# Key norms along turned rows, layer 1 turned by transposes, two bank halves in the scan, another order at its seam

## The chip, the cores and the metric

The kernel runs on one core of a Trainium2 chip. The metric is the device time of one execution in microseconds, as a median of several runs. The engines are TensorE (PE; its weight loads are PEld), VectorE (DVE), ScalarE (ACT), GpSimd (POOL) and SyncE (SP), which issues most of the DMAs.

## The reference

One pass through two layers, on 512 latent tokens and 256 context tokens, D = 1024, all in fp32.

```python
# both layers: scale, shift and gate come from the conditioning vectors by ada_w
u = rms_norm(h, norm_g[i]) * (1.0 + scale) + shift
h = h + gate * mixer(u)

# layer 0, gated DeltaNet in both directions; q, k, v = silu(conv(u @ w_in)), z = the gate path
q = l2_norm(q); k = l2_norm(k)     # x * rsqrt(sum(x * x) + 1e-6) over the 128 of a head
# per chunk of 64 tokens: T = inverse of (I + A), QK = decayed q k^T, and a state S for each head
v_new = T @ (v - k S); o = q S + QK @ v_new; S = S * g + k^T v_new
y = (rms_norm(o) * silu(z)) @ w_out

# layer 1, attention of 8 query heads on 2 key/value heads, with rotary rows; only the latents go on
y_lat = (softmax(q k^T) v * silu(z)) @ w_out
return rms_norm(h_lat, final_norm_g)
```

Layer 0 has 8 key heads and 8 query heads of 128, and 16 value heads of 128.

## The kernel before, in words

Large products run as three passes in a reduced fp32 format: each operand is split into a high part and the rest, and high by high, high by rest and rest by high are summed in PSUM. Times below are us from the start of the profiled span.

**The front (0 to 145)** makes the layer norms, the conditioning and the 8 key heads. For a key head, PE makes the projection in two pieces, of 512 and 256 tokens (`k_products`, L491), with channels on the partitions; ACT and DVE make the convolution and the silu (`sil_k`, 128 channels x 768 tokens). The norm of each token is a sum over partitions. So ACT squares all of it (`k_squared`, L532), PE sums the squares with twelve products by a column of ones, each an fp32 matmul of two instructions (`k_summed`, L540), DVE adds epsilon while it copies the sums out (`k_sums`, L545), and once for two heads DVE takes 1/sqrt (`k_roots`, a chain of small operations, L178 to L183). PE turns the head to tokens on partitions by six transposes (`k_turned`, L461), ACT scales each 128x128 of it by its tokens' roots while it copies it out of PSUM (`k_scaled`, L558, six instructions), the result is stored, and PE turns it back for the second form of the keys (`k_back`, L567; copied by ACT in `k_kept`).

**The heads of q, v and z (145 to 549)** are products of the same kind (`gemm_part`, L929), among them the decay matrices and the inverses T of every chunk (L713 to L892). The last of these are `pn` and `pw` (L846, L864). In both stretches the order of the work on each engine is not written out: each step is a `K(engine, cost, due, function, after=..., takes=..., holds=...)`, and `written_out` (L1113) places them one by one: by the earliest start that the engine, its operands and the free buffers in `pool_of` (L1053) allow, then by due time. `T0` (L1134) and `STEP` set the due times of the key heads, `SLOT` those of the others. Costs only set the order: on the chip every engine takes its own queue in this order and waits on semaphores.

**The scan (549 to 725)** has 48 steps x, four for each chunk, with four heads of both directions each. `products(x)` (L1546 on) makes `ks` on PE (k S and q S), `r` on DVE (L1567, four pieces) and `o` on ACT (L1570, four pieces). `solve(x)` makes `pr` = T r on PE (L1590), and ACT copies it out as `vn` (L1592). `update(x)` makes `pq` = QK vn (L1616), which DVE adds to the output `O` (L1630), and the state's change `su` (L1624), which DVE adds to `S`. `pr` and `pq` have one PSUM buffer of two banks each, of which half is used. A step x of the loop runs `products(x)`, `solve(x - 1)`, `update(x - 2)`. From x = 43 the steps of layer 0's output norm are put between them; `chain` holds the small operations of its roots, and `out_gated`, `out_cast` and `out_rest` (L1703 to L1723) turn the first unit of the output projection into its high part and rest.

**The output projection of layer 0 (725 to 874)** has 32 units n (L1744 three passes each). From n = 24 on, one k at a time, the context tokens are made ready for layer 1: `u_block` is `u_turn` (L1882), then `u_split` (L1887 to L1889). `u_turn` norms and turns in one: a product of `h` with a diagonal matrix `diag1` of the tokens' roots, an fp32 matmul of two instructions for each 128x128. `u_split` applies scale and shift in PSUM on DVE, ACT casts the high part out, and DVE subtracts it. `norm1_diag` makes the diagonal matrices.

**Layer 1 (874 to the end)** begins with `kv`, the keys and values (L2036): six blocks k of the context, then `u_block` for k = 0 and 1 of the latents, then two context blocks, then for each k `u_block(k + 2)` and the latents' `kv_block(k)`. Attention, its gates and the last projection follow. From the scan on the order on PE, DVE and ACT is the order of the code.

Of the kernel before, what the change touches and what calls it, by code (L numbers as in the profile page):

```python
# [8 lines left out]
F32 = mybir.dt.float32  # L9
# [8 lines left out]
P = 128  # L18
# [68 lines left out]
def backbone(tc, a, out):  # L87
# [380 lines left out]
    kw, khl, kbank, kacc, ksil, ksq, kps, kroot, ktr, ktok, kpb = ({} for _ in range(11))  # L468
# [33 lines left out]
    def k_centre(h, i):  # L502
        c0, n = SPAN[i]
        if i == 0:
            open_late()
            kacc[h] = room["late"].tile([P, NTOK], F32, tag="acc", name=f"acc_k{h}", bufs=2)
        S.activation(kacc[h][:, c0:c0 + n], kbank[h, i][:, :n], AF.Copy, scale=cwv[:, 2, 8 + h:9 + h])
# [22 lines left out]
    def k_squared(h):  # L530
        ksq[h] = room["late"].tile([P, NTOK], F32, tag="sq", name=f"sq_k{h}", bufs=2)
        S.activation(ksq[h], ksil[h], AF.Square)  # L532

    def k_summed(h):
        ps = kps[h] = pa.tile([P, 512], F32, tag="gq", name=f"ss_k{h}")
        sq = ksq.pop(h)
        for t in range(NT):
            for hf in range(2):
                c0 = t * P + hf * 64
                T.matmul(ps[hf * 64:hf * 64 + 64, t:t + 1], sq[:, c0:c0 + 64], ones, start=True, stop=True)  # L540

    def k_sums(h):
        if h % 2 == 0:
            kroot[h // 2] = ap_.tile([P, 2 * NT], F32, tag="kss", name=f"kss{h}")
        V.tensor_scalar(kroot[h // 2][:, h % 2 * NT:(h % 2 + 1) * NT], kps.pop(h)[:, 0:NT], EPS, None, ALU.add)  # L545

    def k_roots(h):
        rsqrt(kroot[h // 2], add=False)

# [3 lines left out]
    def k_scaled(h):  # L553
        kt = ktok[h] = room["late"].tile([P, NT, P], F32, tag="tok", name=f"kt{h}", bufs=2)
        pt, r = ktr.pop(h), kroot[h // 2]
        for i, t0, n in halves():
            for t in range(t0, t0 + n):
                S.activation(kt[:, t], pt[i][:, t - t0], AF.Copy, scale=r[:, h % 2 * NT + t:h % 2 * NT + t + 1])  # L558
# [481 lines left out]
    class Piece:  # L1040
        def __init__(self, engine, cost, due, fn, *args, after=(), takes=(), holds=(), lands=0.0, since=0.0, slack=None, behind=(), port=0, sent=0.0, far=0.0):
# [5 lines left out]
            for x, owner in holds:  # L1047
# [8 lines left out]
                                          ("lacc", 2), ("lsil", 4), ("lsq", 2), ("lkb", 2), ("ltok", 2))}  # L1056
# [77 lines left out]
    T0 = 140  # L1134
# [94 lines left out]
    def k_finish(h, e, t0, sown, r_, kown):  # L1229
# [11 lines left out]
    for h in range(QH):  # L1241
# [28 lines left out]
        if h % 2 == 0:  # L1270
            kown, first_of, left_ = ks_, (h, e, t0, sq_[0]), []
            continue
# [1287 lines left out]
```

## Time and profile before

| | |
|---|---|
| median of 3 runs | 1163.69 us (1161.95, 1163.69, 1169.8) |
| the profiled execution, its span | 1162.45 us, 1160.7 us |
| busy share: PE, DVE, ACT, POOL | 97%, 69%, 63%, 51% |
| mean granted TensorE clock | 0.994 |
| PE idle in 0-145, 145-549, 549-725 us | 14.5, 4.7, 4.3 us |
| PE idle in 725-874, 874-917, 917-1127 us, and after | 0.1, 1.7, 3.0, 10.3 us |

The page of the profile gives busy time of each engine and, in 40 slices, the busy share in tenths. A group row reads: line, engine, operation, out<-in, shape, count | busy us, mean ns of one | idle time just before, and what ended it. A timeline row is start, duration, engine, line, operation, out<-in, count; an fp32 matmul or transpose of one call may stand in it as two instructions. Matmuls overlap: the pitch between starts, not the duration, is what each costs PE. The list of waits gives the engine's idle time by what it waited for. A row of windows gives for a stretch its length and then the busy time of PE, PEld, DVE, ACT and POOL, each with its instructions, then the granted TensorE clock, the DMA share and GB/s.

### The profile page before, as it was taken

The numbers are of one execution on the slowest core, as the hardware profiler recorded it, in microseconds if no ns is written. First come the engines' busy times: TensorE is split into PE (matmuls) and PEld (weight loads), VectorE is DVE, ScalarE is ACT, GpSimd is POOL, SyncE is SP. The second block draws the span as 40 slices with busy tenths as digits, with TensorE's granted clock in tenths as the row PEclk, the third lists the DMA queues.
The fourth block names the chain that finished last, engine by engine and source line by source line (L and its number), as shares of the span: only waits on it lengthen the run. The fifth ranks groups of instructions, "written<-read, shape, count | busy, mean of one in ns | idle before, by whom it ended". The sixth has DMA issues, their size and how long they took to land. (4 is left out here: it accounts for less than half of the span.)

```text
span 1160.7 us, 27663 instructions
## 1 busy us (share of the span) xinstructions
PE 1122.1 (97%) x10751; PEld 917.8 (79%) x10751; DVE 796.3 (69%) x1651; ACT 735.2 (63%) x1918; POOL 589.1 (51%) x509
## 2 busy tenths in 40 slices
PE   5999999999999999999999999999999999999996
PEld 2777788888888888887666666788887889999885
DVE  4786465688897888873787888455657467666646
ACT  4545544576876888855789888875753246666731
POOL 0554000149999989930585597556635143130810
PEclk9999999999999999999999999999999999999998
DMA  9577854757647867566988983686844112101323
GB/s 368 200 270 267 302 150 133 220 154 210 180 139 231 265 212 227 171 223 210 268 242 242 285 257 99 205 221 189 250 114 139 34 55 73 37 19 56 109 73 91
DMA packets 117141, 208.73 MB, mean 180 GB/s; under 512 B 12145, under 2 KB 76818, under 8 KB 111762
## 3 DMA queue, kind: packets, MB, share of 16 engines
q1 hardware_dynamic: 97074, 195.32, 54.4%
q10 hardware_dynamic: 19936, 11.64, 3.4%
q8 instruction: 85, 1.39, 0.5%
q14 instruction: 46, 0.38, 0.1%
HBM read 166.16 MB, written 40.67 MB: 178 GB/s over the span
## 5 line engine op out<-in xcount | busy, mean ns | idle before, releaser
L1744 PE MATMUL po<-woh,y 128*128 128x512 f32 x384 | 129.7, 401 | 0.1
L1573 POOL TENSOR_TENSOR S<-S,glb 128x512 f32<-128x512 f32 x80 | 81.8, 1043 | 89.1 <-PE ks L1564 88.8
L1682 POOL TENSOR_TENSOR wol<-wo,woh 128x1024 fp32r<-128x1024 f32 x32 | 77.2, 2412 | 56.0 <-ACT woh L1675 52.7
L813 POOL TENSOR_TENSOR X<-X,tmp 128x62 f32<-128x62 f32 (+15 forms) x93 | 98.1, 1054 | 7.3
L812 POOL TENSOR_TENSOR tmp<-L,X 128x62 f32<-128x62 f32 (+15 forms) x93 | 95.3, 1024 | 6.7
L929 PE MATMUL g_z<-uh,wh_z 128*128 128x512 f32 (+1 forms) x256 | 89.2, 348 | 2.0 <-DVE sil_v L963 1.9
L944 DVE SCALAR_TENSOR_TENSOR acc_v<-g_v,cwv,acc_v 128x510 f32<-128x510 f32 (+3 forms) x128 | 78.0, 614 | 16.4 <-ACT acc_v L936 12.9
L929 PE MATMUL g_v<-uh,wh_v 128*128 128x512 f32 (+1 forms) x256 | 88.0, 344 | 0.0
L929 PE MATMUL g_v<-uh,wl_v 128*128 128x512 f32 (+1 forms) x256 | 86.2, 337 | 1.3 <-issue 1.3
L929 PE MATMUL g_z<-uh,wl_z 128*128 128x512 f32 (+1 forms) x256 | 86.8, 339 | 0.0
L929 PE MATMUL g_z<-ul,wh_z 128*128 128x512 f32 (+1 forms) x256 | 86.7, 339 | 0.0
L929 PE MATMUL g_v<-ul,wh_v 128*128 128x512 f32 (+1 forms) x256 | 86.1, 336 | 0.0
L1744 PEld LDWEIGHTS po<-woh,y 128*128 128x128 f32 x384 | 72.3, 188 | 15.7 <-ACT y L1717 0.3
L1744 PE MATMUL po<-wol,y 128*128 128x512 f32 x192 | 75.4, 393 | 0.0
L1710 DVE SCALAR_TENSOR_TENSOR pt<-pt,og,z 128x128 f32<-128x128 f32 x96 | 34.4, 358 | 33.6 <-PE pt L1701 31.3
L918 POOL TENSOR_TENSOR wl_z<-w_z,wh_z 128x1024 fp32r<-128x1024 f32 x3 | 8.0, 2677 | 96.1 <-ACT wh_z L915 96.1
L1638 DVE TENSOR_TENSOR S<-su,S 128x512 f32<-128x512 f32 x80 | 51.5, 686 | 6.7 <-PE su L1624 4.5
L929 PEld LDWEIGHTS g_z<-uh,wh_z 128*128 128x128 f32 x256 | 48.9, 191 | 8.0 <-DVE sil_v L963 2.2
L1564 PE MATMUL ks<-S,ck 128*64 128x256 f32 x352 | 55.2, 392 | 0.0
L929 PEld LDWEIGHTS g_v<-uh,wl_v 128*128 128x128 f32 x256 | 48.5, 189 | 6.7 <-issue 1.5
L1567 DVE SCALAR_TENSOR_TENSOR r<-ks,negV,cv 128x128 f32<-128x128 f32 x176 | 52.4, 345 | 1.1
L929 PEld LDWEIGHTS g_z<-uh,wl_z 128*128 128x128 f32 x256 | 48.8, 191 | 5.4
(452 smaller groups left out, 3345.0 us busy)
## 6 DMA issues: line engine op xcount, KB each, us to landing
aw<-in_ada_late SPq DMA_DIRECT2D x16, 1024.0 KB, 8.2
wo<-in_dn_w_out SPq DMA_DIRECT2D x32, 512.0 KB, 4.0
cv<-v_d SPq DMA_DIRECT2D x22, 512.0 KB, 8.1
aw<-in_ada_first SPq DMA_DIRECT2D x8, 1024.0 KB, 11.5
w_z<-in_dn_w_in SPq DMA_DIRECT2D x16, 512.0 KB, 5.3
w_v<-in_dn_w_in SPq DMA_DIRECT2D x16, 512.0 KB, 4.2
v_d<-vt ACTq DMA_DIRECT2D x16, 384.0 KB, 4.1
cT<-t_d SPq DMA_DIRECT2D x12, 512.0 KB, 7.7
```

Source lines behind the costliest of these rows:

```text
L812: G.tensor_tensor(tv, bcast(L[:, :, j + 1:, j], 3, j + 1), bcast(X[:, :, j, 0:j + 1], 2, n), ALU.mult)
L813: G.tensor_tensor(X[:, :, j + 1:, 0:j + 1], X[:, :, j + 1:, 0:j + 1], tv, ALU.subtract)
L918: E.tensor_tensor(split_w_[n][1], raw_w.pop(n), split_w_[n][0], ALU.subtract)
L929: T.matmul(ps[:, :m], w[:, k], u[:, k, c0:c0 + m], start=k == 0 and n_ == 0, stop=k == KT - 1 and n_ == 2)
L944: V.scalar_tensor_tensor(acc[:, c0 + lo:c0 + hi], ps[:, lo + j - 2:hi + j - 2], cwv[:, j, ct:ct + 1], acc[:, c0 + lo:c0 + hi], ALU.mult, A ...
L1564: T.matmul(ks[r0:r0 + 64, w], kq[w][:, hh, r0:r0 + 64], St[hh][:, d], start=True, stop=True)
L1567: V.scalar_tensor_tensor(r[:, 2 * j + i], ks[:, 0, i], negV[:, visit, t, h:h + 1], v[:, h], ALU.mult, ALU.add)
L1573: G.tensor_tensor(St[hh], St[hh], bcast(g_, 3, P), ALU.mult)
L1638: V.tensor_tensor(St[hh], sj, St[hh], ALU.add)
L1682: G.tensor_tensor(wl, raws.pop(n), halves[n][0], ALU.subtract)
L1710: V.scalar_tensor_tensor(pj, pj, og, raw(z, off, [[st_, 2], [1, 64]]), ALU.mult, ALU.mult)
L1744: T.matmul(acc[nh], y[i][:, j, :], ww[k][:, nh * 512:(nh + 1) * 512], start=h == 0 and x == 0, stop=h == VH - 1 and x == 2)
```

## The change

It has four parts.

1. **Key norms.** `k_summed` and `k_sums` go. The head is turned first, directly after its silu; ACT then squares each turned 128x128 out of PSUM with an accumulator, which gives the tokens' sums as a column (`k_squared`, six instructions), and copies the turned head out in two wide copies (`k_copied`). The roots follow for two heads at once, now with the epsilon (one DVE operation more), and POOL multiplies the copied head by its roots in place (`k_scaled`, 128x768). `k_back` and the rest stay. The tokens' buffers `tok` go from two to four, `T0` from 140 to 134. Since the list of steps is another, the whole order up to the scan is placed anew.
2. **Layer 1.** `h` is scaled by its roots on ACT ahead of the turn, in wide pieces (`h_columns`): the context in place, 128x512 (n = 22 and 23); the latents 128x128 for k = 0, 128x384 for k = 1 to 3, 128x512 for k = 4 to 7. `u_turn` is then a transpose, one instruction for each 128x128. Scale and shift go from DVE to ACT: one Identity writes the high part, a second one writes the full value in PSUM; DVE still subtracts. `gy` has eight buffers instead of six, which the scaled pieces share.
3. **Bank halves.** `pr` and `pq` are one tile each for the whole scan, and step x takes half x % 2 of it.
4. **Order at the seam.** At x = 47 the last step of the chain and `out_gated`, `out_cast` go from ahead of and within `products(47)` to behind `solve(46)`.

```diff
+    def k_turned(h):
+        ktr[h] = to_tokens(ksil.pop(h), f"k{h}")
+
     def k_squared(h):
-        ksq[h] = room["late"].tile([P, NTOK], F32, tag="sq", name=f"sq_k{h}", bufs=2)
-        S.activation(ksq[h], ksil[h], AF.Square)
-
-    def k_summed(h):
-        ps = kps[h] = pa.tile([P, 512], F32, tag="gq", name=f"ss_k{h}")
-        sq = ksq.pop(h)
-        for t in range(NT):
-            for hf in range(2):
-                c0 = t * P + hf * 64
-                T.matmul(ps[hf * 64:hf * 64 + 64, t:t + 1], sq[:, c0:c0 + 64], ones, start=True, stop=True)
-
-    def k_sums(h):
         if h % 2 == 0:
             kroot[h // 2] = ap_.tile([P, 2 * NT], F32, tag="kss", name=f"kss{h}")
-        V.tensor_scalar(kroot[h // 2][:, h % 2 * NT:(h % 2 + 1) * NT], kps.pop(h)[:, 0:NT], EPS, None, ALU.add)
-
-    def k_roots(h):
...
-    def k_turned(h):
-        ktr[h] = to_tokens(ksil.pop(h), f"k{h}")
...
-    def k_scaled(h):
-        kt = ktok[h] = room["late"].tile([P, NT, P], F32, tag="tok", name=f"kt{h}", bufs=2)
-        pt, r = ktr.pop(h), kroot[h // 2]
         for i, t0, n in halves():
             for t in range(t0, t0 + n):
-                S.activation(kt[:, t], pt[i][:, t - t0], AF.Copy, scale=r[:, h % 2 * NT + t:h % 2 * NT + t + 1])
+                c = h % 2 * NT + t
+                S.activation(ksq[t % 2], ktr[h][i][:, t - t0], AF.Square, accum_out=kroot[h // 2][:, c:c + 1])
+
+    def k_copied(h):
+        kt, pt = room["late"].tile([P, NT, P], F32, tag="tok", name=f"kt{h}", bufs=4), ktr.pop(h)
+        ktok[h] = kt
+        for i, t0, n in halves():
+            S.copy(kt[:, t0:t0 + n], pt[i][:, :n])
+
+    def k_roots(h):
+        rsqrt(kroot[h // 2])
+
+    def k_scaled(h):
+        kt, r = ktok[h], kroot[h // 2]
+        G.tensor_tensor(kt, kt, bcast(r[:, h % 2 * NT:(h % 2 + 1) * NT], 2, P), ALU.mult)
...
-    T0 = 140
+    T0 = 134
...
-        tu = K("PE", 0.65, t0 - 20, k_turned, h, after=[r_], takes=["tr", "tr"], holds=[("lsil", sown)], lands=0.1, slack=QUICK)
-        sc_ = K("ACT", 2.2, e + 8, k_scaled, h, after=[tu, r_], takes=["ltok"], holds=[("tr", tu), ("tr", tu), ("kss", kown)], lands=0.1)
...
+        sc_ = K("POOL", 1.85, e + 8, k_scaled, h, port=1, after=[r_, cp_], holds=[("ltok", cp_), ("kss", kown)], lands=0.1)
...
+        tu = K("PE", 0.65, t0 - 50, k_turned, h, after=si + backs.pop(h - 4, []), takes=["tr", "tr"], holds=[("lsil", sq_[0])], lands=0.1, slack=QUICK)
+        ks_ = K("ACT", 2.9, e + 6, k_squared, h, after=[tu], takes=["kss"] if h % 2 == 0 else (), holds=[("tr", tu), ("tr", tu)] + ([("kss", kown)] if h % 2 else []), lands=0.1)
+        cp_ = K("ACT", 1.0, e + 7, k_copied, h, after=[tu, ks_], takes=["ltok"], holds=[("tr", tu), ("tr", tu)], lands=0.1)
...
-        r_ = K("DVE", 2.1, e + 6, k_roots, h, port=9, after=[ks_, kown], holds=[("kss", kown)], lands=0.1)
...
+        r_ = K("DVE", 2.3, e + 6, k_roots, h, port=10, after=[ks_, kown], holds=[("kss", kown)], lands=0.1)
...
+        prq = [pcx.tile([P, 2, 4, P], F32, tag=tag, name=f"{tag}_all", bufs=1) for tag in ("pr", "pq")]
...
-            pr_ = pcx.tile([P, 2, 4, P], F32, tag="pr", name=f"pr{x}", bufs=1)
+            pr_ = prq[0][:, :, x % 2 * 2:x % 2 * 2 + 2]
...
             vn = ch.tile([P, 4, P], F32, tag="vn", name=f"vn{x}", bufs=2)
-            S.copy(vn.rearrange("p (j i) d -> p j i d", j=2), pr_[:, :, 0:2])
+            S.copy(vn.rearrange("p (j i) d -> p j i d", j=2), pr_)
...
-            po = pcx.tile([P, 2, 4, P], F32, tag="pq", name=f"pq{x}", bufs=1)
+            po = prq[1][:, :, x % 2 * 2:x % 2 * 2 + 2]
...
-        if x == 47:
-            out_gated(0, AB)
         if x < 48:
             products(x)
         if x == 45:
             out_scale(0, AB)
-        if x == 47:
-            out_cast(0, AB)
         if 0 <= x - 1 < 48:
             solve(x - 1)
         if x == 47:
+            some(chain, 99)
+            out_gated(0, AB)
+            out_cast(0, AB)
             out_rest(0, AB)
             out_scale(0, C)
         if 0 <= x - 2 < 48:
...
         if x in (43, 44, 45, 46):
-            some(chain, (3, 6, 6, 99)[x - 43])
+            some(chain, (3, 6, 6, len(chain) - 1)[x - 43])
...
+        gy = acc if inside else hpool.tile([P, 512], F32, tag="gy", name=f"gy{t}_{nh}", bufs=8)
...
-    def norm1_diag(tiles, r):
+    hn = {}
+
+    def h_columns(k0, k1, tiles, r):
         for t in tiles:
-            S.activation(diag1[t], ident, AF.Copy, scale=r[:, t - min(tiles):t - min(tiles) + 1])
+            h, m = h_t[t][:, k0 * P:k1 * P], (k1 - k0) * P
+            if t < 2:
+                y = h
+            elif k1 == 1:
+                if t == 2:
+                    hn["t"] = hpool.tile([P, 4, P], F32, tag="hn", name="hn")
+                y = hn["t"][:, t - 2]
+            else:
+                y = hpool.tile([P, 512], F32, tag="gy", name=f"hn{k0}_{t}", bufs=8)[:, 0:m]
+            S.activation(y, h, AF.Copy, scale=r[:, t - r0[t]:t - r0[t] + 1])
+            for k in range(k0, k1):
+                hn[k, t] = y[:, (k - k0) * P:(k - k0 + 1) * P]
...
         ps = trt(f"ht{k}_{j}")
         for q, t in enumerate(tiles):
-            T.matmul(ps[:, q, :], h_t[t][:, k * P:(k + 1) * P], diag1[t], start=True, stop=True)
+            T.transpose(ps[:, q, :], hn[k, t], ident)
         return ps.rearrange("p a b -> p (a b)")[:, 0:len(tiles) * P]
 
     def u_split(k, j, pv, dst):
 
-        V.tensor_scalar(pv, pv, au[1][:, j, 1, k:k + 1], au[1][:, j, 0, k:k + 1], ALU.mult, ALU.add)
-        S.copy(dst[0][:, k], pv)
+        s_, b_ = au[1][:, j, 1, k:k + 1], au[1][:, j, 0, k:k + 1]
+        S.activation(dst[0][:, k], pv, AF.Identity, bias=b_, scale=s_)
+        S.activation(pv, pv, AF.Identity, bias=b_, scale=s_)
         V.tensor_tensor(dst[1][:, k], pv, dst[0][:, k], ALU.subtract)
...
-        if n == 22:
-            norm1_diag((0, 1), r_c)
+        if n in (22, 23):
+            for k0 in (0, 4):
+                h_columns(k0, k0 + 4, (n - 22,), r_c)
...
-    norm1_diag((2, 3, 4, 5), r_l)
+    h_columns(0, 1, lat, r_l)
+    h_columns(1, 4, lat, r_l)
...
+            u_block(k + 2, 0, lat, uL)
+        if k < 2:
+            h_columns(4, 8, lat[2 * k:2 * k + 2], r_l)
         kv_block(k, (2, 3, 4, 5))
```

What the built programs show of it, in the order of the queues (numbers behind names tell tiles apart):

ACT in the front, key head 0. Before, from the square on (`sq_k`, then the six scaled copies `kt`):

```order
L532 ACTIVATE sq_k_1014<-sil_k_935 128x768
L558 ACTIVATE kt_1045<-tr_k_1016,kss_790 128x128 x4
L558 ACTIVATE kt_1045<-tr_k_1017,kss_790 128x128 x2
L507 ACTIVATE acc_k_1012<-g_k_999,cwv 128x256
L520 ACTIVATE g_k_904<-acc_k_1012 128x512
L485 CAST wh_k_1096<-w_k_881 128x1024
L576 COPY kb_1121<-kb_0_1101 128x512
L576 COPY kb_1121<-kb_0_1102 128x256
```

Now, from the first square on:

```order
L542 ACTIVATE sq_k_545,kss_698<-tr_k_672 128x128
L542 ACTIVATE sq_k_546,kss_698<-tr_k_672 128x128
L542 ACTIVATE sq_k_545,kss_698<-tr_k_672 128x128
L542 ACTIVATE sq_k_546,kss_698<-tr_k_672 128x128
L542 ACTIVATE sq_k_545,kss_698<-tr_k_673 128x128
L542 ACTIVATE sq_k_546,kss_698<-tr_k_673 128x128
L423 COPY rows_4_721<-pa_4_689 128x512
L548 COPY kt_731<-tr_k_672 128x512
L548 COPY kt_731<-tr_k_673 128x256
L485 CAST wh_k_749<-w_k_670 128x1024
```

The square of 128x768 and the six scaled copies have become six squares of 128x128 with an accumulator (`kss`) and two wide copies, which stand earlier, ahead of the roots.

DVE at the seam of scan and output projection, x = 47, from the chain's last step (`fo`) on. Before:

```order
L1486 SCALAR_TENSOR_TENSOR fo<-fo,rq 128x16
L1710 SCALAR_TENSOR_TENSOR pt_9898<-pt_9898,og,z_0_9246 128x128 x2
L1567 SCALAR_TENSOR_TENSOR r_9903<-ks_0_9905,negV,cv_9707 128x128 x2
L1567 SCALAR_TENSOR_TENSOR r_9903<-ks_1_9914,negV,cv_9707 128x128 x2
L1723 TENSOR_TENSOR y_0_0_9925<-pt_9898,y_0_0_9924 128x256
L1630 TENSOR_TENSOR O_7010<-pq_9940,O_7010 128x512
```

Now, from `r` of step 47 on:

```order
L1565 SCALAR_TENSOR_TENSOR r_9713<-ks_0_9715,negV,cv_9526 128x128 x2
L1565 SCALAR_TENSOR_TENSOR r_9713<-ks_1_9724,negV,cv_9526 128x128 x2
L1483 SCALAR_TENSOR_TENSOR fo<-fo,rq 128x16
L1708 SCALAR_TENSOR_TENSOR pt_9710<-pt_9710,og,z_0_9079 128x128 x2
L1721 TENSOR_TENSOR y_0_0_9748<-pt_9710,y_0_0_9747 128x256
L1628 TENSOR_TENSOR O_6912<-pq_all,O_6912 128x512 x2
```

`r` of step 47 has moved ahead of `fo` and the gating (`pt`), and the two additions to `O` (L1628; of `pq` of steps 45 and 46) stay behind `y`, the rest of the first unit. On PE, with the semaphores of each row, the change has there `pr` of step 47, `pq` of step 46 and the first products of the output projection:

```order
L1588 MATMUL pr_all_6943<-r47_9713,cT_11_9525 64x128 [waits DVE_49,Activation_49]
L1588 MATMUL pr_all_6943<-r47_9713,cT_11_9525 64x128
L1588 MATMUL pr_all_6943<-r47_9713,cT_11_9525 64x128 [waits DVE_49]
L1588 MATMUL pr_all_6943<-r47_9713,cT_11_9525 64x128 x3
L1588 MATMUL pr_all_6943<-r47_9713,cT_11_9525 64x128 [waits DVE_49]
L1588 MATMUL pr_all_6943<-r47_9713,cT_11_9525 64x128
L1614 MATMUL pq_all_6944<-vn46_9742,cQK_11_9527 64x128 [waits DVE_49]
L1614 MATMUL pq_all_6944<-vn46_9742,cQK_11_9527 64x128 x7
```

`pr` of step 47 still waits for ACT: the copy `vn46`, which reads the other half. `pq` of step 46 still waits for DVE: the addition just ahead of it, of `pq` of step 45, which reads the other half as well. So stand these waits through the whole scan.

PE in layer 1, the first two turns of the latents. Before:

```order
L1882 MATMUL ht_0_11662<-dn_10038,h_10023 128x128
L1882 MATMUL ht_0_11662<-dn_10039,h_10024 128x128
L1882 MATMUL ht_0_11662<-dn_10040,h_10025 128x128
L1882 MATMUL ht_0_11662<-dn_10041,h_10026 128x128
L1882 MATMUL ht_0_11670<-dn_10038,h_10023 128x128
L1882 MATMUL ht_0_11670<-dn_10039,h_10024 128x128
L1882 MATMUL ht_0_11670<-dn_10040,h_10025 128x128
L1882 MATMUL ht_0_11670<-dn_10041,h_10026 128x128
L2036 MATMUL kv_11589<-wkv_10030,uC_10032 128x512
```

Now:

```order
L1892 MATMUL ht_0_11475<-ident,hn 128x128 x4
L1892 MATMUL ht_0_11483<-ident,hn_2_11423 128x128
L1892 MATMUL ht_0_11483<-ident,hn_3_11425 128x128
L1892 MATMUL ht_0_11483<-ident,hn_4_11427 128x128
L1892 MATMUL ht_0_11483<-ident,hn_5_11429 128x128
L2048 MATMUL kv_11393<-wkv_9838,uC_9840 128x512
```

Half as many instructions, and the second turn (`ht_0_11483`) now reads the 128x384 pieces (`hn_2` to `hn_5`), which ACT makes after the four of 128x128 that the first turn reads. Both still stand ahead of the context's last two blocks of `kv`.

More of the change, by code (lines that the diff above doesn't have):

```diff
@@ L506, in k_centre @@
             kacc[h] = room["late"].tile([P, NTOK], F32, tag="acc", name=f"acc_k{h}", bufs=2)
+            if h == 0:
+                for j in range(2):
+                    ksq[j] = room["late"].tile([P, P], F32, tag=f"sq{j}", name=f"sq_k{j}")
         S.activation(kacc[h][:, c0:c0 + n], kbank[h, i][:, :n], AF.Copy, scale=cwv[:, 2, 8 + h:9 + h])
@@ L1861, in load_h @@
             dma(h_t[t][hf * 64:hf * 64 + 64, :], src[c * 64:c * 64 + 64, :])
-    diag1 = [hpool.tile([P, P], F32, tag=f"dn{t}", name=f"dn{t}") for t in range(NT)]
     def norm1_steps(tiles, nm):
```

39 lines of the change are left out of this document (18 added, 21 removed).

## The prediction

> **What bounds the kernel now.** I read the busy times first, then TensorE's list of waits, then windows and the timeline of the places that the change touches. The page begins:
>
> ```profile
> span 1160.7 us, 27663 instructions
> ## 1 busy us (share of the span) xinstructions
> PE 1122.1 (97%) x10751; PEld 917.8 (79%) x10751; DVE 796.3 (69%) x1651; ACT 735.2 (63%) x1918; POOL 589.1 (51%) x509
> ```
>
> PE has 38.6 us of idle time in the whole span. So an instruction taken off PE is worth its pitch wherever PE is never idle, and work moved to ACT, DVE or POOL is free until PE waits for it. The list of PE's waits (us in total, times, longest) has these that touch the change:
>
> ```profile
> PE pr L1590 <- ACT vn L1592: 3.0, 2, 1.7
> PE g_z L929 <- DVE sil_v L963: 1.9, 1, 1.9
> PE ht L1882 <- DVE uL L1889: 1.3, 2, 1.1
> PE g_v L929 <- issue: 1.3, 1, 1.3
> PE pw L864 <- issue: 1.0, 1, 1.0
> ```
>
> Two windows of the key heads show what PE and the others do there:
>
> ```profile
> 58.00:87.00 29.00, 29.00 (x232) 21.97 (x231) 25.95 (x52) 12.23 (x22) 16.58 (x18) 1.00 0.77 271
> 87.00:116.00 29.00, 29.00 (x240) 22.53 (x239) 19.94 (x50) 14.78 (x38) 14.09 (x31) 1.00 0.76 267
> ```
>
> PE is busy for all 29 us of both; ACT has half of the time free, POOL 12 to 15 us, DVE only 3 us in the first.
>
> **Key norms, PE: -7.0 us.** The eight groups of sums go; the turn of each head stays, only earlier. The group of sums over PE instructions, and one of the eight blocks in the timeline, between a product and the next other one:
>
> ```profile
> L540 PE MATMUL ss_k<-ones,sq_k 128*64 128x1 f32 x192 | 6.9, 199 | 0.0
> ```
>
> ```profile
> 72.85 0.28 PE L500 MATMUL g_k<-ul,wh_k 128*128 128x256 f32 x1
> 73.06 0.87 PE L540 MATMUL ss_k<-ones,sq_k 128*64 128x1 f32 x24
> 73.86 0.70 PE L431 MATMUL pg<-rows,sel 128*128 128x512 f32 x1
> ```
>
> The products before it go at a pitch of 0.12, so the next would have come at 72.97; it came at 73.86. A block costs between 0.80 (its own start to the next) and 0.89: 6.4 to 7.1 for eight. I take 7.0, near the group's 6.9 busy.
>
> What replaces them must stay hidden. ACT, by rows of the same forms:
>
> ```profile
> L532 ACT ACTIVATE sq_k<-sil_k 128x768 f32<-128x768 f32 x8 | 6.8, 846 | 2.2 <-DVE sil_k L528 2.2
> L558 ACT ACTIVATE kt<-tr_k,kss 128x128 f32<-128x128 f32 x48 | 13.3, 381 | 5.2 <-PE tr_k L461 5.2
> L1592 ACT COPY vn<-pr 128x512 f32<-128x512 f32 x48 | 28.2, 588 | 2.9 <-PE pr L1590 1.3 <-DVE sil_z L961 0.9 <-ACT O L1628 0.7
> ```
>
> A head has cost 0.85 + 13.3/8 = 2.5. Now it has six squares with an accumulator and copies of 512 and 256 columns. If a square takes no more than a scaled copy of its size with its read-out 0.1 longer (0.28 to 0.38), that is 1.7 to 2.3, with copies of 0.59 and about 0.4: 2.7 to 3.3, up to 0.8 a head more, some 6 us in a stage of 60 in which ACT is half idle. POOL's 128x768 product is new. The nearest row is the scan's 128x512:
>
> ```profile
> L1573 POOL TENSOR_TENSOR S<-S,glb 128x512 f32<-128x512 f32 x80 | 81.8, 1043 | 89.1 <-PE ks L1564 88.8
> ```
>
> By columns that is 1.6 a head. It is hidden by the products of about two heads, which the new order puts between a head's turn and its `kb`. DVE loses a copy for each head and gains an operation for each pair. So the stage's sum is PE's.
>
> **The order placed anew: 0, from -3.6 to +4.** All of the stage up to 549 is placed anew, and its waits with it; those in the list that are likely to go or come are the 1.9, 1.3 and 1.0. The 1.9 has a tail. The timeline at it, and windows behind it (granted clock third from the end):
>
> ```profile
> 341.38 0.82 PE L461 MATMUL tr_v<-ident,sil_v 128*128 128x128 f32 x6
> 344.14 0.50 PE L929 MATMUL g_z<-uh,wh_z 128*128 128x512 f32 x1 [1.94 <-DVE sil_v L963]
> ```
>
> ```profile
> 344.00:346.00 2.00, 1.86 (x7) 1.55 (x8) 2.00 (x2) 1.56 (x4) 1.20 (x2) 0.86 0.89 293
> 346.00:348.00 2.00, 2.00 (x6) 1.52 (x6) 2.00 (x5) 1.97 (x7) 1.70 (x1) 0.50 1.06 241
> 348.00:350.00 2.00, 2.00 (x9) 1.60 (x8) 2.00 (x2) 1.54 (x7) 1.84 (x4) 0.79 1.07 343
> ```
>
> After 2.76 us with nothing but six transposes on PE the clock fell to a half: 2 x (0.14 + 0.50 + 0.21) = 1.7 us lost. With the wait that is 3.6, the most that this place can give back. In the new order the silu for which PE waited no longer stands behind a mask product, but DVE is as full there as before, and other heads now stand where none waited. One such stall fewer or one more is as likely: I take 0.
>
> At the stage's end the last half of `pw` now has only 24 products of 256 columns behind it, at 0.12 each 2.9 us, ahead of the scan's first `pr`. The chunk's queries `cq` take over its memory, so their load moves there:
>
> ```profile
> 537.35 0.32 SPq L1537 DMA_DIRECT2D cq<-q_d  x1
> ```
>
> ```profile
> 549.27 0.67 PE L1590 MATMUL pr<-cv,cT 64*64 64x128 f32 x16
> 555.86 0.65 PE L1564 MATMUL ks<-S,ck 128*64 128x256 f32 x4
> ```
>
> ```profile
> cv<-v_d SPq DMA_DIRECT2D x22, 512.0 KB, 8.1
> cq<-q_d SPq DMA_DIRECT2D x11, 512.0 KB, 4.8
> ```
>
> It was issued 11.9 us ahead of `pr` and will be at about 2.8; first use is 6.6 after `pr`. Landing in 4.8 to 8.1 leaves 4.6 to 1.3 us: no wait, by a small margin.
>
> **Bank halves: 0.** The most that they could free is the 3.0 of `pr` for `vn`. But the built program makes `pr` of each step wait for the copy of the other half, and `pq` for the addition, as before: the halves of both banks interleave, and the order in which PE meets these waits is unchanged.
>
> **Seam: +0.5, from -0.9 to +0.7.** The timeline of DVE, ACT and PE around x = 47:
>
> ```profile
> 720.88 0.74 DVE L1710 SCALAR_TENSOR_TENSOR pt<-pt,og,z 128x128 f32<-128x128 f32 x2
> 721.53 1.12 DVE L1567 SCALAR_TENSOR_TENSOR r<-ks,negV,cv 128x128 f32<-128x128 f32 x4
> 724.03 0.68 DVE L1630 TENSOR_TENSOR O<-pq,O 128x512 f32<-128x512 f32 x1
> ```
>
> ```profile
> 724.20 0.67 PE L1590 MATMUL pr<-r,cT 64*64 64x128 f32 x16 [1.68 <-ACT vn L1592]
> 724.77 0.67 PE L1616 MATMUL pq<-vn,cQK 64*64 64x128 f32 x16
> ```
>
> With `r` first, `r`, `o` and `vn` come about 0.7 earlier and `pr` starts at about 723.5. But the chain's last step (0.9), the gating (0.65 to 0.74), ACT's cast and the rest (0.4 each) now stand on DVE ahead of the addition for which `pq` waits: 722.25 + 0.9 + 0.65 + 0.5 + 0.4 + 0.65 = 725.35, where `pq` had started at 724.77. What `pr` gains `pq` gives back, and 0.5 more. If the halves freed `pq`, this would be -0.9.
>
> **Layer 1: -5.1 us.** A turn on the chain of waits, beside its products, and the fp32 form of before:
>
> ```profile
> 896.62 0.89 PE ht L1882 x8
> 897.51 2.80 PE kv L2036 x12
> ```
>
> Four 128x128 cost 0.89 as eight instructions; the `tr_v` row above has six transposes in 0.82, a pitch of 0.11, so 0.44 for four. Eight context turns of two save 0.22 each, in a stage in which PE idles 0.1 of 149 us: 1.8. The latents at the seam, on PE and ACT:
>
> ```profile
> 882.45 2.21 PE L1882 MATMUL ht<-dn,h 128*128 128x128 f32 x16 [0.38 <-issue]
> 884.42 3.00 PE L2036 MATMUL kv<-wkv,uC 128*128 128x512 f32 x12
> 888.55 1.13 PE L1882 MATMUL ht<-dn,h 128*128 128x128 f32 x8 [1.13 <-DVE uL L1889]
> 889.44 3.06 PE L2036 MATMUL kv<-wkv,uL 128*128 128x512 f32 x12
> ```
>
> ```profile
> 881.95 1.28 ACT L1876 ACTIVATE dn<-ident,hrl 128x128 f32<-128x128 f32 x4 [2.45 <-DVE hrl L203]
> ```
>
> The first turn needs four scaled pieces of 128x128, like the four diagonals: until 883.2. The second needs four of 128x384, which at 0.46 (by width between 0.32 and 0.59) end at 885.1, a wait of 1.5 that is new. Behind it on PE stand the context's last 12 products: 885.4 to 888.2, no wait for the third turn (1.13 before), and the latents' products at 888.6 instead of 889.4: -0.8. Five more turns at -0.45 and the 0.2 wait of k = 3: -2.5. Together -3.3. ACT has two Identities (1.2), two scaled pieces (1.2) and key squares (1.1) in the first rounds, 3.5 against PE's 3.24: tight for two rounds, then free.
>
> In the new wait, PE holds only eight transposes between 882.1 and 885.4. [...]
>
> **The sum:** -7.0 - 1.8 - 3.3 + 0.5 = -11.6 on the profiled execution's 1162.45 (span 1160.7 and 1.75 around it), 1150.9, say 1151. The median stands 1.2 above that execution, so by medians it could be 1152.
>
> **The rivals.** *A stall fewer:* the wait at 344 goes with its tail and nothing comes for it: -3.6, 1147.5. For it speaks the silu's new place; against it a DVE busy all the time there. *Clock at layer 1:* the gap between 882 and 885 halves the clock as at 344, 1.7 more, 1152.6. For it speaks the likeness; against it that the eight transposes come in two groups, with a wait after each no longer than 1.7, like the wait for `vn` above, which has no slow window behind it. *New waits:* a head of the new order waits as at 344, or `cq` lands later than 8.1 us after its issue: +4, 1155. For it speaks the margin of 1.3; against it the median of 4.8. *Key heads bound by POOL:* the scaling of a head waits behind POOL's and DVE's own work, `kb` stands in PE's order, and PE waits at every head. At 1.45 us a head the whole gain is gone, at 0.8 with the clock's tail of 1.7 on half of them; at 2 us a head it gives 1167. For it speaks that DVE has 3 us free of 29 between 58 and 87 and that POOL enters the chain of every head; against it that POOL has 12 us free in the same window and two heads' products stand between. *The halves do what they say:* 1.4 at the seam and 1.3 at the scan's start: 1148.
>
> **How the numbers follow.** Forecast 0.46, a stall fewer 0.16, clock 0.12, new waits 0.17, POOL 0.05, halves 0.04. The forecast's own range, with the bounds of sums and seam, is 1149 to 1153. 1% of the median, about what a measurement of this kernel can tell from no change, puts the bound at 1152.05: two thirds of the forecast's cases, a stall fewer, the halves and a quarter of the clock give 0.53 for faster; POOL gives 0.04 for slower; the rest, 0.43, is same. The range of 8 in 10 goes from 1147 (a stall fewer) to 1157 (new waits).
>
> **What would show it.** In the profile after: no `ss_k`, and PE still at 29 of 29 us in both windows of the key heads; waits of `kb` for POOL would mean the POOL rival. `ht` as transposes at 0.44, with a wait of about 1.5 for ACT ahead of the second turn of the latents, and none before the third. Still a wait of `pr` for `vn` near 549 and before the output projection, there near 1.0, followed by one of `pq` for DVE: without it the halves work. A granted clock below 1.00 at layer 1's seam, or a wait of `ks` for `cq`, would each name its rival. The prediction is wrong if PE waits over 4 us anew before 549, or if the gain lies elsewhere than in these three stages.

## The result, and the profile after

The change takes 1151.14 us (median of 4 runs, 1150.85 to 1153.66); the kernel before, beside it, 1166.09 (4 runs, 1161.95 to 1169.8). The ratio is 0.9891, interval 0.9867 to 0.9914: faster, by about 1%, where 1151 had been forecast. One run of all those below, of the change without its key norms, took 1388.53 at a granted clock of 0.75 and is left out of the ratios. The profiled execution took 1150.85, span 1148.9, 11.8 less than before. The page after begins:

```profile
span 1148.9 us, 27237 instructions
## 1 busy us (share of the span) xinstructions
PE 1110.4 (97%) x10511; PEld 905.9 (79%) x10511; DVE 787.1 (69%) x1631; ACT 749.9 (65%) x2000; POOL 599.5 (52%) x517
```

PE has lost 240 instructions and 11.7 us of busy time, as much as the span. Its list of waits, of those that touch the change:

```profile
PE pr_all L1588 <- ACT vn L1590: 2.2, 2, 1.3
PE pp L837 <- issue: 2.1, 1, 2.1
PE g_z L926 <- issue: 1.6, 2, 0.9
...
PE pq_all L1614 <- DVE O L1628: 1.4, 1, 1.4
PE pq_all L1614 <- issue: 1.1, 1, 1.1
...
PE ht L1892 <- ACT hn L1882: 0.7, 4, 0.2
PE ht L1892 <- DVE ksq L176: 0.7, 1, 0.7
```

The 1.9 for `sil_v` is gone; a 2.1 in `pp` has come, in which the profile names no releaser, as well as the `pq` wait for DVE, the turns' waits for ACT, and waits without a releaser in `g_z` and, in the scan, in `pq`. `kb` isn't in the list. The key heads' windows:

```profile
58.00:87.00 29.00, 29.00 (x193) 21.53 (x192) 25.25 (x58) 14.69 (x47) 16.70 (x19) 1.00 0.80 286
87.00:116.00 29.00, 29.00 (x200) 21.98 (x199) 16.91 (x35) 14.58 (x43) 12.48 (x25) 1.00 0.91 307
```

PE is still busy for all of both. To see where the 11.8 us came from I cut both traces at the same four places of the program (start of the scan's first `pr`, of the first `po`, `kv` and `pg` of `z`; us):

| stretch | before | after | difference | by the prediction |
|---|---|---|---|---|
| up to the first `pr` | 549.27 | 538.88 | -10.4 | -7.0 |
| scan, to the first `po` | 176.18 | 177.63 | +1.4 | +0.5 |
| output projection, to the first `kv` | 148.27 | 146.96 | -1.3 | -1.8 |
| `kv`, to the first `pg` | 43.60 | 42.14 | -1.5 | -3.3 |
| the rest | 243.38 | 243.29 | -0.1 | 0 |

The total is the forecast's (-11.6); the stages are not. 3.4 more came from ahead of the scan, and 3.2 less from behind its start. The experiments had to say what made each of the two.

### The profile page after: what moved, and what is told of

Its sections match the earlier page's. It is cut to its first block, busy times and chain, and to the rows that moved or that the text cites. A ratio compares the mean times of both kernels' runs of the same rounds, so it can differ in the third digit from the quotient of the medians.

```text
span 1148.9 us, 27237 instructions
## 1 busy us (share of the span) xinstructions
PE 1110.4 (97%) x10511; PEld 905.9 (79%) x10511; DVE 787.1 (69%) x1631; ACT 749.9 (65%) x2000; POOL 599.5 (52%) x517
## 4 chain that ended last, share of the span: by engine, by line
PE 89%; DVE 4%; issue 3%; ACT 2%; POOL 1%; DMA 1%; ACTq 0%; POOLq 0%; DVEq 0%
PE g_z L926 12%; PE g_v L926 12%; PE po L1742 8%; PE ks L1562 7%; PE g_k L500 6%; PE g_q L926 6%; PE pg L2167 4%; PE su L1622 3%; PE pg L2218 3%; PE po L2287 3%; PE s L2238 3%; PE pr_all L1588 2%; PE pa L316 2%; PE kv L2048 2%; PE pq_all L1614 2%
## 5 line engine op out<-in xcount | busy, mean ns | idle before, releaser
L810 POOL TENSOR_TENSOR X<-X,tmp 128x62 f32<-128x62 f32 (+15 forms) x93 | 101.0, 1086 | 7.3
L809 POOL TENSOR_TENSOR tmp<-L,X 128x62 f32<-128x62 f32 (+15 forms) x93 | 90.2, 970 | 6.7
L941 DVE SCALAR_TENSOR_TENSOR acc_v<-g_v,cwv,acc_v 128x510 f32<-128x510 f32 (+3 forms) x128 | 77.8, 614 | 15.2 <-ACT acc_v L933 11.4
L555 POOL TENSOR_TENSOR kt<-kt,kss 128x768 f32<-128x768 f32 x8 | 11.6, 1472 | 85.6 <-DVE kss L183 57.1
L926 PEld LDWEIGHTS g_z<-ul,wh_z 128*128 128x128 f32 x256 | 48.8, 191 | 6.5 <-issue 1.9
L1562 PE MATMUL ks<-S,cq 128*64 128x256 f32 x352 | 53.6, 379 | 0.0
```

The source lines that it names most:

```text
L809: G.tensor_tensor(tv, bcast(L[:, :, j + 1:, j], 3, j + 1), bcast(X[:, :, j, 0:j + 1], 2, n), ALU.mult)
L810: G.tensor_tensor(X[:, :, j + 1:, 0:j + 1], X[:, :, j + 1:, 0:j + 1], tv, ALU.subtract)
L926: T.matmul(ps[:, :m], w[:, k], u[:, k, c0:c0 + m], start=k == 0 and n_ == 0, stop=k == KT - 1 and n_ == 2)
L941: V.scalar_tensor_tensor(acc[:, c0 + lo:c0 + hi], ps[:, lo + j - 2:hi + j - 2], cwv[:, j, ct:ct + 1], acc[:, c0 + lo:c0 + hi], ALU.mult, A ...
L1562: T.matmul(ks[r0:r0 + 64, w], kq[w][:, hh, r0:r0 + 64], St[hh][:, d], start=True, stop=True)
```

## The experiments

All are told by the same cuts. For each part alone, the diff is that part of the change's own diff.

Executions of equal code differ, and the traces show by how much. Seven of them have the change's order of PE up to the scan (the change, the key norms alone, POOL twice, the second turn later, the addition ahead, no halves, both reorderings): their first `pr` starts between 536.13 and 538.88. The two with the order of before have 549.27 and 548.35. So what came from ahead of the scan is 9.5 to 13.1, and a single start is not read closer than about 3 us.

**The key norms alone** (the kernel before with `k_turned` to `k_scaled`, the list of steps and `T0 = 134`).

> The kernel before with the key norms' part alone. Its queues up to the scan are those of the change, row for row. If the parts add up by stage, the scan's first pr starts at 538.9 +- 0.5 us (549.3 before), the rest takes as long as before (611.4), and the span is 1150.3, so by itself this part is nearly the whole gain (ratio 0.991). Rival, that the parts share the gain as the prediction's terms had it (7.0 of 11.6): span 1153.7.

Measured: 1153.71 us (6 runs) against 1164.05, ratio 0.9913 (0.9881 to 0.9945); span 1151.1. The first `pr` starts at 537.83, the scan takes 179.03 with the old seam (3.55 from `pq` of step 45 to the first `po`, as before), output projection 148.16, `kv` 42.74. So this part gives 11.4 ahead of the scan and loses 2.9 within it, 2.1 of it a wait of `pq` without a releaser. By the ratio it is nearly the whole gain, as the first expectation had it, but the start of `pr` and the rest (613.3 instead of 611.4) lie outside its bounds. The stretch of `kv` is 0.9 shorter than before though nothing was changed there: by so much can that stage differ too, so the parts add up by stage only roughly.

**Everything but the key norms.**

> The change without the key norms' part: layer 1, bank halves and seam order. If the stages add up as the two traces have them, the first pr stays at 549.3, the stretch from there to the first po is 0.7 longer (176.9), the output projection 1.3 shorter, the stretch of kv 1.5 shorter with the granted clock at a half for about 3 us: span 1158.6, about the same as before by runs. Rival, the prediction's terms for these parts (-1.8, -3.3, +0.5): span 1156.1, with the clock at 1.00 throughout layer 1.

Measured: 1162.09 us (10 runs) against 1164.05, ratio 0.9973 (0.9948 to 0.9999): 0.3%, by an interval that all but touches 1; span 1157.7. First `pr` 548.35, scan 176.15, output projection 148.28, `kv` 41.58. Neither expectation came whole: the output projection is not shorter, since a wait of 1.0 of `pt` for `y` came, and `kv` is 2.0 shorter with the clock at 1.00. The turns there are those of the change; what differs is the products behind them. In the change:

```profile
874.31 0.33 PE L1892 MATMUL ht<-ident,hn 128*128 128x128 f32 x1 [0.18 <-ACT hn L1882]
874.81 0.47 PE L1892 MATMUL ht<-ident,hn 128*128 128x128 f32 x1 [0.18 <-ACT hn L1882]
874.94 4.47 PE L2048 MATMUL kv<-wkv,uC 128*128 128x512 f32 x12
```

And without the key norms:

```profile
883.62 0.33 PE L1895 MATMUL ht<-ident,hn 128*128 128x128 f32 x1 [0.18 <-ACT hn L1885]
884.12 0.33 PE L1895 MATMUL ht<-ident,hn 128*128 128x128 f32 x1 [0.18 <-ACT hn L1885]
884.21 3.00 PE L2051 MATMUL kv<-wkv,uC 128*128 128x512 f32 x12
```

The same turns wait for the same pieces, one by one, with starts 0.5 apart; the twelve products behind take 4.47 in one execution and 3.00 in the other. (Behind these, the third turn waits 0.76 for `uL` here, which the change doesn't.) The windows of the change there show the granted clock (third from the end):

```profile
874.00:876.00 2.00, 1.64 (x6) 1.13 (x6) 0.93 (x3) 2.00 (x5) 1.31 (x2) 0.67 0.01 2
876.00:878.00 2.00, 2.00 (x6) 1.59 (x5) 1.27 (x2) 1.39 (x3) 2.00 (x1) 0.50 0.00 0
```

This is the rival on the clock. Eight profiled executions of this document have the same rows of turns: five lost the clock behind them (the change, the sums put back, no halves, `T0` 140 and 128), three did not. And the wait from which the prediction took the price stands in this kernel too, with the same 1.94 behind the same six transposes, but without its tail:

```profile
344.38 0.50 PE L929 MATMUL g_z<-uh,wh_z 128*128 128x512 f32 x1 [1.94 <-DVE sil_v L963]
```

```profile
344.00:346.00 2.00, 1.61 (x7) 1.36 (x8) 2.00 (x2) 1.56 (x4) 1.35 (x3) 1.00 0.91 248
346.00:348.00 2.00, 2.00 (x11) 1.65 (x10) 2.00 (x5) 1.97 (x6) 1.42 (x1) 1.00 1.03 292
```

So such a gap costs 1.7 us more in some executions and nothing in others. The pause in `pp`, 1.9 to 2.4 us, has slow clock behind it in three of the seven executions that have it at the same product. Why the same gap loses the clock in some executions only, no run here shows. What the traces show is for how long: in all thirteen, half clock comes in stretches of 3.41 us or twice that (526.52 to 529.93 and 874.68 to 878.09 in the change), but for the last, which runs to the end.

**The sums put back** behind each turn, their result unread:

```diff
+        ps = pa.tile([P, 512], F32, tag="gq", name=f"ss_k{h}")
+        for t in range(NT):
+            for hf in range(2):
+                c0 = t * P + hf * 64
+                T.matmul(ps[hf * 64:hf * 64 + 64, t:t + 1], s[:, c0:c0 + 64], ones, start=True, stop=True)
```

> The change with the twelve products by a column of ones of each key head put back on PE, behind its turn, their result unread; nothing else differs on any engine. If the sums were on PE's path at their whole price, the first pr comes 7.0 us later by the prediction's term (545.9), or 7.8 later if each block also makes the next product 0.1 late (0.98 a block; 546.7). Rival, that a good part of the 10.4 us before the scan came from the order placed anew: under 5 later.

Measured: the first `pr` at 543.60, 4.7 later than in the change: under 5, as the rival had it, but 4.7 to 7.5 later than in the seven executions of that order, so the start alone doesn't decide. The busy time of PE up to there is closer to the price: 526.94 against 520.92. The clock cost 1.2 more in this execution's first 30 us and 1.6 less at `pp` (where the change lost it, below), so the sums cost 6.0 - 1.2 + 1.6 = 6.4, 0.80 a head. PE's other waits were 1.3 shorter, which is the rest: 6.4 + 1.2 - 1.6 - 1.3 = 4.7. The kernel before agrees: there each of the eight blocks takes 0.80 from its first product to the next other one. So do six of the eight here; two rows show one of the two others, at 0.94:

```profile
66.47 0.87 PE L540 MATMUL ss_k<-ones,sil_k 128*64 128x1 f32 x24
67.41 1.06 PE L316 MATMUL pa<-aw,sc 128*32 128x512 f32 x8
```

**POOL twice:**

```diff
+        G.tensor_scalar(kt, kt, 1.0, None, ALU.mult)
```

> The change with a second pass of POOL over each scaled key head (times 1.0, in place), in the same order on all engines, so that POOL takes about 1.5 us longer for each head. If POOL's step is hidden by the products between a head's turn and its kb, no wait of kb for POOL appears and the first pr stays at 538.9 +- 0.6. Rival (key heads bound by POOL, or nearly so): PE waits at kb, up to 1.5 us at each of eight heads, first pr up to 12 later.

Measured: the first `pr` at 538.40, 0.5 earlier than in the change; no wait of `kb` in the list. The added pass was even longer than meant (groups of POOL in the front, five of the eight heads):

```profile
L556 POOL TENSOR_SCALAR kt<-kt 128x768 f32<-128x768 f32 x5 | 10.7, 2136 | 0.4
L555 POOL TENSOR_TENSOR kt<-kt,kss 128x768 f32<-128x768 f32 x5 | 7.4, 1473 | 47.3 <-issue 24.1 <-DVE kss L183 23.2
```

3.6 us of POOL a head is hidden as well as 1.5. The rival that POOL binds the key heads falls.

**The second turn later:**

```diff
-    for k in range(2):
-        u_block(k, 0, lat, uL)
+    u_block(0, 0, lat, uL)
     for k in range(6, KT):
         kv_block(k, (0, 1))
+    u_block(1, 0, lat, uL)
```

> The change with the second turn of the latents (k = 1) put behind the context's last two blocks of kv, nothing else. If the gap on PE is made by that turn waiting for ACT's 128x384 pieces, the waits of ht for hn go (0.7 in four pieces in the change), the products follow the first turn at once, the granted clock stays at 1.00 there, and the stretch from the first kv to the first pg takes 39.5 to 40.5 us instead of 42.1. Rival, that ACT is the bound of the stretch: the waits come back at k = 2 to 4, and it takes 41 or more even at full clock.

Measured: `kv` to `pg` takes 39.90; span 1146.7. PE there:

```profile
871.88 1.21 PE L1892 MATMUL ht<-ident,hn 128*128 128x128 f32 x4
872.85 2.98 PE L2048 MATMUL kv<-wkv,uC 128*128 128x512 f32 x12
875.67 0.60 PE L1892 MATMUL ht<-ident,hn 128*128 128x128 f32 x4
876.87 0.66 PE L1892 MATMUL ht<-ident,hn 128*128 128x128 f32 x4 [0.60 <-DVE uL L1900]
877.28 3.04 PE L2048 MATMUL kv<-wkv,uL 128*128 128x512 f32 x12
```

The waits for `hn` are gone and the clock stays at 1.00. The latents' products start 5.4 us after the first turn instead of 7.7. Of these 2.3, the clock is 1.4; the other 0.9 is the wait. A wait of 0.6 for the rest of k = 1 is new. So the gap came from the turn's place in PE's queue, not from ACT's work as such.

**The addition ahead of the gating:**

```diff
+        if 0 <= x - 2 < 48:
+            update(x - 2)
         if x == 47:
-            some(chain, 99)
             out_gated(0, AB)
...
-        if 0 <= x - 2 < 48:
-            update(x - 2)
...
-            some(chain, (3, 6, 6, len(chain) - 1)[x - 43])
+            some(chain, (3, 6, 6, 99)[x - 43])
```

> The change with another order at x = 47: the addition of pq of step 45 goes ahead of the gating, the chain's last step back to x = 46. If pq of step 46 waited only for that addition behind the gating, the 1.4 wait of pq for DVE goes, and from pq of step 45 to the first po it takes 2.7 to 3.0 us (4.24 in the change, 3.55 before). Rival, that y, the rest of the first unit, is what ends last: 3.5 or more, the wait now in front of po.

Measured: 3.10 from `pq` of step 45 to the first `po`; span 1144.6. PE at the seam, in the change and then here:

```profile
713.77 0.67 PE L1588 MATMUL pr_all<-r,cT 64*64 64x128 f32 x16 [0.88 <-ACT vn L1590]
715.83 0.67 PE L1614 MATMUL pq_all<-vn,cQK 64*64 64x128 f32 x16 [1.39 <-DVE O L1628]
716.51 0.49 PE L1742 MATMUL po<-woh,y 128*128 128x512 f32 x1
```

```profile
711.82 0.67 PE L1588 MATMUL pr_all<-r,cT 64*64 64x128 f32 x16 [0.87 <-ACT vn L1590]
712.30 0.62 PE L1614 MATMUL pq_all<-vn,cQK 64*64 64x128 f32 x16
713.38 0.30 PE L1699 MATMUL pt<-ident,so 128*128 128x128 f32 x1 [0.46 <-DVE y L1721]
713.43 0.48 PE L1742 MATMUL po<-woh,y 128*128 128x512 f32 x1
```

`pq` follows `pr` at once; `y` ends last, but only by 0.46, a little over what was expected. In the change DVE's queue read

```profile
712.43 1.22 DVE L1483 SCALAR_TENSOR_TENSOR fo<-fo,rq 128x16 f32<-128x16 f32 x1
713.57 0.74 DVE L1708 SCALAR_TENSOR_TENSOR pt<-pt,og,z 128x128 f32<-128x128 f32 x2
714.75 0.42 DVE L1721 TENSOR_TENSOR y<-pt,y 128x256 fp32r<-128x256 f32 x1 [0.44 <-ACT y L1715]
715.09 0.68 DVE L1628 TENSOR_TENSOR O<-pq_all,O 128x512 f32<-128x512 f32 x1
```

with the addition behind all of the gating, as the prediction had it.

**No halves** (the change with `pr` and `pq` as one tile a step, as before).

> The change with one buffer of pr and pq a step as before, instead of the halves. If the halves free nothing, since the copies and additions still hold both banks, the waits of pr for vn (2.2) and pq for O (1.4) stay within 0.1, the seam from pq of step 45 to the first po stays at 4.24, and the scan up to that pq at 172.3 plus whatever waits with no releaser come. Rival, that they free something: 0.4 to 0.7 longer up to there, as the two kernels without halves had it (172.5 and 172.6 against 171.9 to 172.3).

Measured: the waits are 2.2 and 1.4 again, the seam 4.25. From the first `pr` to `pq` of step 45 it takes 175.32, of which 2.8 are waits that the change doesn't have (three without a releaser, 1.3, and one of `ks` for ACT, 1.5); without them 172.5. In the change it is 173.39, less its 1.1 without a releaser 172.25. The two waits say that the halves free nothing there; 0.2 or 0.3 is no more than the executions of equal code differ by, so the smaller rival isn't shown.

**Other due times for the key heads,** one number in the change and in the kernel before:

```diff
-    T0 = 134
+    T0 = 140
```

> The change with T0 left at 140, so that the same steps are placed in another order from the first query head on. If what the order adds to the sums' price (10.4 measured before the scan, 6.4 for the sums) is chance of placement, the first pr moves by 1 to 4 us either way, with other waits in the list. If the key heads' due times do it, it comes 2 to 4 later (541 to 543) with the waits unchanged in kind.

> The change with T0 at 128 instead of 134: the order of the same steps from the first heads on is once more another. If the time by T0 is chance of placement (134: first pr at 538.9, 140: 544.2 and 10 more in the scan), it comes out between 1145 and 1165 with waits at other places. If earlier due times help as such, the first pr is at 533 to 537.

> The kernel before with T0 at 134, nothing else. If the due time alone makes the order better, its first pr comes 2 to 4 us earlier (545 to 547 instead of 549.3), which would be the part of the change's 10.4 that the sums don't explain. If placement is chance, it may as well come later, with new waits: 548 to 560.

Measured, one execution each (the first `pr`, the span, with the two kernels of the study for comparison):

| | first `pr` | span |
|---|---|---|
| change, `T0` 128 | 552.04 | 1174.4 |
| change, `T0` 134 | 538.88 | 1148.9 |
| change, `T0` 140 | 544.21 | 1164.1 |
| before, `T0` 134 | 550.91 | 1166.4 |
| before, `T0` 140 | 549.27 | 1160.7 |

With `T0` at 140 the same four parts are not faster than the kernel before at all (1166.02 us, one run, beside 1164.37). Waits of that run that the change doesn't have:

```profile
PE pr_all L1588 <- ACT vn L1590: 4.6, 2, 3.7
PE g_z L926 <- DVE wl_z L915: 4.5, 1, 4.5
...
PE su L1622 <- issue: 3.0, 1, 3.0
PE ks L1562 <- ACT O L1568: 2.9, 1, 2.9
```

and at 128:

```profile
PE g_z L926 <- DVE sil_v L960: 4.6, 1, 4.6
...
PE su L1622 <- issue: 2.5, 1, 2.5
PE ks L1562 <- DMA cq<-q_d: 2.4, 1, 2.4
```

Each new order brings stalls at other places, and with them slow clock: between the first 30 us and the last stretch, half clock lasts 17 us at 140 and 27 at 128, 6.8 in the change. An earlier due time doesn't help as such: the three points of the change don't lie on a slope, and the kernel before doesn't gain the 2 to 4 us that were expected if it did. That it loses isn't shown: the spans of its own runs beside these experiments go from 1157.6 to 1171.5. This 128 run also shows the wait of `ks` for `cq` that the prediction feared at the scan's start.

**Both reorderings,** of the turn and of the addition:

> The change with both reorderings of the runs before it: the second turn of the latents behind the context's last blocks of kv, and the addition ahead of the gating at x = 47. If each acts in its own place, from pq of step 45 to the first po it takes 3.1 us and from the first kv to the first pg 39.9, with the clock at 1.00 there: against the change -1.1 and -2.2, a span of 1143 to 1146, ratio to before 0.983 to 0.985 and at least 0.2% below the change. Rival, that what is gained at the seam comes back as a wait in the first units of the output projection: that stage over 148 (147.0 in the change).

Measured: 1149.43 us (6 runs, 1147.04 to 1150.62), ratio 0.9872 (0.9847 to 0.9897); span 1145.1, with 175.92 for the scan, 147.07 and 39.94 for the next two stages. The stages do what each did alone, and the seam's gain doesn't come back behind it. The span is within what was expected; the ratio (0.983 to 0.985) is not. The profiled span is 3.8 below the change's, of which 1.4 was the change's clock in layer 1. The interval of the ratio overlaps the change's, so the runs alone don't show it to be faster than the change; both are faster than the kernel before.

## Why the prediction was right

**Key norms, -7.0.** The place and the cover were right: PE had no idle time (29.00 us busy of 29.00 in both windows), ACT, POOL and DVE hid the rest, with a second pass of POOL still hidden. The price was the lower end of the row's own range: 6.4 instead of 7.0, since a block costs 0.80 where PE changes its kind of product anyway: the last transpose of a turn takes 0.20, those ahead of it 0.11, both ahead of sums in the kernel before and ahead of `pa` in the change. The run that shows it has the sums behind the turns; between pieces of the projection, where some stood before, they also made the products beside them longer (at 72.85 the last product ahead of a block took 0.21 instead of 0.12; those behind, below).

**The order placed anew, 0.** This is the step that failed in size and, above all, in its bounds. Of the 10.4 ahead of the scan 4.0 are not the sums: 1.2 is less waiting (17.96 us idle instead of 19.18, with `pp` for `sil_v`), the tail of slow clock only moved from 345 to 526 (1.7 and 1.6), and 2.8 is other busy time of PE, of which 0.9 stands at `g_k`, whose first product behind a block of sums took longer (in the kernel before 0.22 instead of 0.12 with 256 columns, 0.33 instead of 0.23 with 512). Some of this 0.9 is thus the sums' too, and then 7.0 was no worse a price than 6.4. The remaining 1.9 is spread over `kb`, `tr_v`, `g_v` and others, 0.4 at most at each, less 0.7 at `pg`; why was not tested. In the six other executions of the new order the tail at 526 came in two. That the sum of the list of waits is as likely to fall as to rise was a fair guess for this order. The bounds, -3.6 to +4, were those of one stall; the orders for `T0` 140 and 128, with the same work in them as the change, show +15 and +26 on its span. The wait and its clock tail were taken as belonging together, which the run without key norms refutes (the same 1.94, with the clock at 1.00 behind it).

**The scan's first loads.** `cq` did land in time. But in the change the loads between 540 and 580 take longer to land than in the 40 us of the same place before (`cv` 10.8 us against 7.5, `cQK` 9.7 against 5.5), and at 576 PE stands still for 1.1 us within a group of `pq`:

```profile
576.00 0.38 PE L1614 MATMUL pq_all<-vn,cQK 64*64 64x128 f32 x3 [1.14 <-issue]
```

The same pause was 0.4 to 2.1 in five of the six other runs of this order; POOL twice has none there, and neither has a run of the old order. The later loads need not be its cause: it stands at the place of PE's queue at which 50 of 53 such pauses stand (last section). It is none of the waits that the prediction's rival "new waits" named. All new waits of PE ahead of 549, by which the prediction was to be judged wrong if over 4 us, are 3.7 in the change (`pp`, `g_z`): close to it.

**Bank halves, 0.** Right: the waits are the same with the halves as without them (2.2 of `pr` for `vn` and 1.4 of `pq` for `O` in both). The reason given, that the halves interleave over two banks, was not shown: no run here laid them out otherwise.

**Seam, +0.5.** Measured 4.24 - 3.55 = +0.7, by the path that was worked out: `pr` 0.8 earlier against its wait, `pq` 1.4 late behind the gating. Another part shows one stage later: the turn of the next unit waits for `y` (0.2 in the change, 1.0 in the run without key norms).

**Layer 1, -5.1.** The context turns cost 0.13 instead of 0.37 at their place, -1.9 for eight as predicted (-1.8), but the stage got only -1.3: 0.2 of the rest is the wait just named, and 0.3 that its products `po` took longer. A latents' turn of four costs 0.35, less than the 0.44 forecast. Yet the latents got -1.5 instead of -3.3, because the rival on the clock came true in this execution; where it did not, the stretch took 40.6 (POOL twice, the addition ahead), -3.0, or 41.6 with one more wait (without the key norms). The rival had been given 0.12 and came in five of eight.

So it was luck that the sum was right within 0.2 us. It stood on one term 4.0 too small ahead of the scan, set against 0.6 too much for the sums and 3.2 for what came behind: the clock 1.4 to 1.7, the pause in the scan 1.1, the rest small. What was right is the mechanism of the key norms and of the seam, and that PE's own instructions set the time (1110.4 us busy of 1148.9, and 11.7 of the 11.8 gained).

## What to carry to other kernels

When a change alters a planner's input, its new order is a cost of its own: try neighbouring values of a number that only moves the order, with all else equal, before a gain is put down to the change. A wait that is moved off one engine's queue can come back behind the next entry of another, as at the seam (`pr` 0.8 earlier, `pq` 1.4 late): list what stands between the moved step and the next thing that PE waits for. And give PE something other than a few transposes to do where it waits for a neighbour; a turn placed behind the products that don't need it brought 2.2 us against the change, and 0.7 against the executions that had kept the clock.

## What was not expected of the hardware

The same gap on PE, with the same rows, was followed by 3.4 us of half clock in five of eight executions, and the 1.94 us wait near 344 in one of two: a price of 1.7 us that is paid by chance. And PE pauses for about 2 us in the middle of the 128 small products of `pp`, of which in the program only the first carries a wait:

```profile
523.93 0.44 PE L837 MATMUL pp<-U,mo 32*32 32x32 f32 x28
526.52 1.59 PE L837 MATMUL pp<-U,mo 32*32 32x32 f32 x100 [2.15 <-issue]
```

In all seven runs with the same PE stream up to there it stands at the same product, 28 of 128 done, and takes 1.9 to 2.4 us; with 192 more products ahead of it, the sums put back, it came with 37 left instead of 100. So it depends on the place in the instruction stream.

The traces show which place. Number the rows of PE's queue (matmuls, weight loads and the rows of semaphores). Behind the first 30 us, the thirteen traces have 53 pauses of PE of over 0.3 us without a releaser, and 50 of them stand 193 or 194 rows behind a multiple of 256: those in `pp`, the one at 576, and those of `g_v` and `pw` in the kernel before. The other three stand at the fp32 turns `ht`. The 192 products with their weight loads are 384 rows, one and a half such blocks, and they moved the pause by half a block. The page also lists a queue that brings instructions (packets, MB, share):

```profile
q8 instruction: 83, 1.36, 0.5%
```

That is one packet of 16 KB for about 256 of the change's 21324 rows, and one of them starts 0.6 us ahead of the pause in `pp`. So it seems that PE waits there for its next block of instructions. This is read from the places alone; no run here changed how they are loaded, and at most borders of such blocks PE doesn't pause (in the change it does so for over 0.3 us at four of some 80).
